# SwiGLU's transposed result: from TensorE transposes to VectorE block transposes and GpSimd moves in 13 of 22 blocks

## The chip, the cores and the metric

One core of a Trainium2 chip runs the kernel. The metric is device time in microseconds (us), the median of repeated runs. Five engines matter: PE (TensorE, matmuls), DVE (VectorE), ACT (ScalarE), POOL (GpSimd) and SP (SyncE, which issues the loads). Each works through its own queue in the order in which the instructions stand there, and waits at an instruction until what it needs is done.

## The reference

One decoder layer on 256 tokens of width 2048: a SwiGLU half step, a mixing layer, another SwiGLU half step, each with norms and a conditioning vector. Cut to what the change touches:

```python
D_MODEL = 2048; SEQ = 256; D_FF = 5632

def swiglu(h, w_gate, w_up, w_down):
    return (jax.nn.silu(h @ w_gate) * (h @ w_up)) @ w_down
# x: (1, 256, 2048) float32; gate and up: (2048, 5632), down: (5632, 2048), all float32
```

The conditioning vector is multiplied with `w_ada` (2048 x 18432), a stream of its own beside the layer's weights.

## The kernel before

**Tiles.** All products keep float32 accuracy by three matmuls (`mm3`): a value is split into a rounded high part and a rest, and high times high, high times rest and rest times high are added in PSUM. A weight tile is 512 KB (2 x 128 rows of 512 columns). `load_w` has SP load it into one of 8 slots of the pool `rawp` (tag `raw`); `split_w` has ACT cast it to `wh` (L315) and DVE subtract to get `wl` (L320), into one of 4 pairs. PE then runs 12 matmuls of it (2 row halves, 2 token halves, 3 products), lines L338 to L340. A slot of `rawp` is free once the subtraction has read it. The tiles of `w_ada` use the same 8 slots; DVE accumulates them (L172).

**Blocks.** A feed-forward step (FFN0 at the start, FFN1 at the end) has 11 blocks of 512 hidden columns. A block runs gate's tiles, then up's tiles, both with the 128 tokens of a half on partitions, into two PSUM banks each (`gb[t]`, `ub[t]`). Blocks are grouped into supers; after the blocks of a super come its tiles of `w_down`. FFN0's supers are blocks 8, 5, 6, 7; then 0, 1, 2, 3; then 4, 9, 10. FFN1's are 4, 4 and 3 blocks. Most blocks have 16 row tiles of 128, that is 8 weight tiles for gate and 8 for up. In FFN0 blocks 0 to 4 some of the rows were done earlier and their sums lie in SBUF (`part`): 12 rows are left, 6 tiles for gate and 6 for up, and `swiglu_sum` adds the stored part. `swiglu_evac` does the other blocks.

**SwiGLU's result.** For each token half t, ACT takes Silu of gate and DVE multiplies by up. In `swiglu_evac` Silu (L551) reads gate's PSUM bank, and DVE multiplies (L552). In `swiglu_sum` DVE first adds the stored part to gate (L564), ACT takes Silu (L565), DVE adds the stored part to up (L566) and multiplies (L567). The down product needs this with hidden columns on partitions, so `to_g` transposes: 8 PE transposes of 128x128 (L542), in two groups of four, each group into one PSUM bank, from which ACT casts (L373) and DVE subtracts (L374).

**What sets the order.** Steps that are to run beside the weight stream are generators in `pending`; one step runs after each weight tile (`pump`). A tile scheduler then settles each engine's order, bound by data and by `behind(instruction, other)`, which keeps an instruction after another on its engine. `floor[0]` (DVE) and `floor[1]` (ACT) name the instruction that every later `wl` and `wh` must stand behind.

Of the kernel before, what the change touches and what calls it, by code (L numbers as in the profile page):

```python
# [8 lines left out]
F32 = mybir.dt.float32  # L9
F32R = mybir.dt.float32r  # L10
AF = mybir.ActivationFunctionType
# [3 lines left out]
P = 128  # L15
D = 2048
S = 256
NT = S // P
# [14 lines left out]
def tile_layer(  # L33
# [6 lines left out]
    nc = tc.nc  # L40
# [14 lines left out]
    rawp = ctx.enter_context(tc.tile_pool(name="rawp", bufs=8))  # L55
# [9 lines left out]
    def nm(s):  # L65
        uid[0] += 1
        return f"{s}_{uid[0]}"

    def ps():
        return psp.tile([P, 512], F32, tag="ps", name=nm("ps"))  # L70

    def t2(shape=(P, 512), dtype=F32):
        return tp.tile(list(shape), dtype, tag="t2", name=nm("t2"))
# [63 lines left out]

    last_split = [None]
    first_splits = [2]
    floor = [None, None]  # L140
    last_update = [None]

    def behind(ins, other):

        if other is not None:
            tc.add_manual_dep(ins.ins, other.ins.name, mybir.DependencyInfo(
                mybir.DependencyClass.NoSync, mybir.DependencyReason.DATA), reason="order")
# [129 lines left out]
    pending = []  # L277
# [17 lines left out]
    def flush():  # L295
        while pending:
            pump()
# [10 lines left out]
    def split_w(rawv, slot, w):  # L308
        if slot is None:
            wh = wsp.tile([P, 2, 512], F32R, tag="wh", name=nm("wh"))  # L310
            wl = wsp.tile([P, 2, 512], F32R, tag="wl", name=nm("wl"))
        else:
            wh, wl = slot[:, 0], slot[:, 1]
        wh, wl = wh[:, :, 0:w], wl[:, :, 0:w]
        behind(nc.scalar.copy(wh, rawv), floor[1])  # L315
        if first_splits[0]:
            first_splits[0] -= 1
            nc.gpsimd.tensor_tensor(out=wl, in0=rawv, in1=wh.bitcast(F32), op=ALU.subtract)
            return wh, wl
        last_split[0] = nc.vector.tensor_tensor(out=wl, in0=rawv, in1=wh.bitcast(F32), op=ALU.subtract)  # L320
        behind(last_split[0], floor[0])
        return wh, wl
# [49 lines left out]
    def split_act(dh, dl, src):  # L372
        act = nc.scalar.copy(dh, src)  # L373
        return nc.vector.tensor_tensor(out=dl, in0=src, in1=dh.bitcast(F32), op=ALU.subtract), act  # L374


    def parts():

        p = small((P, 8), "parts")
        nc.gpsimd.memset(p[:, 3:4], EPS)  # L380
        return p
# [151 lines left out]
        return banks, 2  # L533


    def to_g(g, gts):
        for i in range(2):
            pg = ps()
            for j in range(2):
                for t in range(NT):  # L540
                    m = 2 * i + j
                    nc.tensor.transpose(pg[:, j * S + t * P:j * S + (t + 1) * P], gts[t][:, m * P:(m + 1) * P], ident)  # L542
            split_act(g.t[:, 0, 2 * i:2 * i + 2, :], g.t[:, 1, 2 * i:2 * i + 2, :],
                      pg.rearrange("p (k s) -> p k s", s=S))
            yield

    def swiglu_evac(g, gb, ub):
        gts = []
        for t in range(NT):
            sg, gt = t2(), t2()  # L550
            nc.scalar.activation(sg, gb[t], AF.Silu)  # L551
            nc.vector.tensor_tensor(out=gt, in0=sg, in1=ub[t], op=ALU.mult)  # L552
            gts.append(gt)
        yield
        yield
        yield from to_g(g, gts)

    def swiglu_sum(gb, ub, part):

        pv = part.t.rearrange("p k s -> p (k s)")  # L560
        gts = []
        for t in range(NT):
            sg, gt = t2(), t2()
            nc.vector.tensor_tensor(out=sg, in0=pv[:, t * 512:(t + 1) * 512], in1=gb[t], op=ALU.add)  # L564
            nc.scalar.activation(sg, sg, AF.Silu)  # L565
            nc.vector.tensor_tensor(out=gt, in0=pv[:, 1024 + t * 512:1024 + (t + 1) * 512], in1=ub[t], op=ALU.add)  # L566
            nc.vector.tensor_tensor(out=gt, in0=sg, in1=gt, op=ALU.mult)  # L567
            gts.append(gt)
        part.free()
        g = Slot((P, 2, 4, S), F32R)  # L570

        def rest():
            yield
            yield
            yield from to_g(g, gts)

        pending.append(rest())
        return g

    def ffn(idx, supers, begun, xin, nxt, nxt_src=None, nxt_c0=None, nxt_w=512):  # L580

        y = None
        yp = [parts() for _ in range(NT)]

        def evac_y(si, q, t, bank):
            ys = y[t].t[:, q * 512:(q + 1) * 512]
            if si == 0:
                nc.scalar.copy(ys, bank)
            else:
                nc.vector.tensor_tensor(out=ys, in0=ys, in1=bank, op=ALU.add)  # L590
            if si == len(supers) - 1:
                sumsq(yp[t], q, ys)

        for si, blocks in enumerate(supers):
            gs = []
            n = len(blocks)
            for b, segs, part, banks in blocks:
                if si == 0 and begun is not None and not gs:
                    gb = proj_tok(w_ff_gate[idx], b * FB, begun)
                    ub = proj_tok(w_ff_up[idx], b * FB)  # L600
                elif part is not None:
                    gb = proj_tok(w_ff_gate[idx], b * FB, segs=segs, first=segs[0][0])
                    ub = proj_tok(w_ff_up[idx], b * FB, segs=segs, first=segs[0][0])
                    flush()
                    gs.append(swiglu_sum(gb, ub, part))
                    continue
                else:
                    gb = proj_tok(w_ff_gate[idx], b * FB, segs=segs, banks=banks and banks[0])
                    ub = proj_tok(w_ff_up[idx], b * FB, segs=segs, banks=banks and banks[1])
                flush()  # L610
                gs.append(Slot((P, 2, 4, S), F32R))
                pending.append(swiglu_evac(gs[-1], gb, ub))
            if y is None:
                y = [Slot((P, D)) for _ in range(NT)] if xin[0].__class__ is Half else [Half(t) for t in range(NT)]
            rows = [(4 * i, 4, 4 * b[0]) for i, b in enumerate(blocks)]

            def mms(k, wh, wl, t):
                g = gs[k // 4].t
                mm3(banks[t], g[:, 0, k % 4, t * P:(t + 1) * P], g[:, 1, k % 4, t * P:(t + 1) * P],
                    wh, wl, k == 0, k == 4 * n - 1)  # L620

            for q in range(4):
                banks = [ps(), ps()]
                if si == len(supers) - 1 and q == 2:
                    for s_ in xin:
                        s_.t
                if si == len(supers) - 1 and q == 3:
                    flush()
                    if side[0] is not None:
                        side[0].drain()  # L630
                    early = early_w(nxt_src, nxt_c0, nxt_w)
                    kept, slots = hold(w_ff_down[idx], rows, q * 512, NW if nxt is None else 3)

                    def last_mm(t):
                        for k, wh, wl in kept:
                            mms(k, wh, wl, t)

                    return boundary(last_mm, lambda t: evac_y(si, q, t, banks[t]), lambda t: times_gg(y, t, q), xin, y, yp, slots + gs,
                                    early, 1, nxt, nxt_src, nxt_c0, nxt_w)
                else:  # L640
                    for k, wh, wl in w_tiles(w_ff_down[idx], rows, q * 512):
                        for t in range(NT):
                            mms(k, wh, wl, t)
                    for t in range(NT):
                        later(evac_y, si, q, t, banks[t])
                        if si == len(supers) - 1:
                            later(times_gg, y, t, q)
            if si < len(supers) - 1:
                for g in gs:
                    g.free()  # L650
# [68 lines left out]
    for bs, n in (((0, 1, 2, 3, 4), 1), ((5, 6), 2), ((7,), 3)):  # L719
        first.until(n - 1)  # L720
        for b in bs:
            part = Slot((P, 8, S))
# [5 lines left out]
    banks = [proj_tok(gate_up[u], 8 * FB, segs=FULL[:3]) for u in range(2)]  # L728
# [25 lines left out]

    blocks = [(4718, 410), (4308, 410), (3896, 412), (3484, 412), (G0, 412)]
    begun = ffn(0, supers, None, xin, 1, w_in, *blocks[0])
    side[0] = None

# [58 lines left out]
    for i, (c0, w) in enumerate(blocks):  # L817
        banks = proj_tok(w_in, c0, begun if i == 0 else None, w)
# [147 lines left out]
    for i in range(2):  # L966
        banks = proj_t(w_in, i * 512)
# [72 lines left out]
    for i in range(2):  # L1040
        banks = proj_tok(w_in, O0 + i * 512)
# [44 lines left out]
    for q in range(4):  # L1086
        banks = b0 if q == 0 else [ps(), ps()]
# [55 lines left out]
```

## Time and profile before

| what | value |
|---|---|
| median of 3 runs | 1872.48 us (1872.23 to 1872.91) |
| the profiled execution, whole time | 1872.83 us |
| its span from first to last instruction | 1870.8 us |
| PE busy | 1823.0 us, 97% of the span |
| DVE busy | 1365.0 us |
| ACT busy | 853.6 us |
| POOL busy | 22.5 us |

Times of rows are microseconds from the span's start. An engine's row gives when an instruction began, how long it took, its line and its tiles, and in brackets how long the engine was idle before it and what ended that. Rows begin a little before the preceding one ends where the engine takes them in as a pipeline, so the step from start to start is what a sequence costs.

### The profile page before, as it was taken

Reading aid. Unit: us, or ns where it says so; the run is one execution under the profiler, and the core shown is the slowest. Engines: PE = TensorE matmul, PEld = TensorE weight load, DVE = VectorE, ACT = ScalarE, POOL = GpSimd, SP = SyncE. Lnnn points to the kernel's source line nnn. Section 1 sums busy time; section 2 is a strip of 40 time slices with the busy share of each in tenths; the row PEclk is TensorE's granted clock in tenths of the full one; section 3 lists DMA queues with packets and bytes.
Section 4 is the critical chain, followed back from the end, with each engine's and each line's share of the span. In section 5 each row is a group of like instructions: output and inputs, shape, how many; then the busy total and the mean of one; then the engine's idle time right before and its main releaser. Section 6 shows DMA issues by size and latency. Waiting matters only on the chain.

```text
span 1870.8 us, 23057 instructions
## 1 busy us (share of the span) xinstructions
PE 1823.0 (97%) x8501; PEld 1523.7 (81%) x8501; DVE 1365.0 (73%) x1479; ACT 853.6 (46%) x1058; POOL 22.5 (1%) x42
## 2 busy tenths in 40 slices
PE   3999999999999999999999999999999999999998
PEld 2888888888888888799988887888888888888886
DVE  6888798788987888868898987555556555556455
ACT  3555444444443444655545446444444444334443
POOL 1000000000000000000000000000000000000000
PEclk9999999999999999999999999999999999999999
DMA  9999889999899999578689994776677776677662
GB/s 346 346 359 342 314 293 318 319 307 322 294 331 323 340 306 334 188 240 278 218 288 306 358 342 141 221 223 213 228 228 221 221 223 214 219 228 220 190 190 91
DMA packets 232617, 499.82 MB, mean 267 GB/s; under 512 B 16828, under 2 KB 28332, under 8 KB 231992
## 3 DMA queue, kind: packets, MB, share of 16 engines
q1 hardware_dynamic: 232504, 498.36, 79.9%
q8 instruction: 66, 1.08, 0.2%
q14 instruction: 47, 0.39, 0.1%
HBM read 496.19 MB, written 2.10 MB: 266 GB/s over the span
## 4 chain that ended last, share of the span: by engine, by line
PE 86%; issue 8%; DVE 3%; DMA 2%; POOL 1%; ACT 0%; DVEq 0%; POOLq 0%; ACTq 0%; SPq 0%
PE ps L338 28%; PE ps L339 28%; PE ps L340 28%; DVE acc L172 2%; PE ps L542 1%; DVE wl L320 1%; DMA raw<-in_w_ada_dram 1%; DMA raw<-in_w_ff_up_dram 0%; POOL rstd L391 0%; DMA raw<-in_w_ff_gate_dram 0%; DMA xt<-in_x_dram 0%; PE ps L197 0%; PE ps L930 0%; ACT wh L315 0%; POOL brs L808 0%
## 5 line engine op out<-in xcount | busy, mean ns | idle before, releaser
L320 DVE TENSOR_TENSOR wl<-raw,wh 128x1024 fp32r<-128x1024 f32 (+2 forms) x635 | 766.1, 1210 | 450.3 <-ACT wh L315 449.3
L315 ACT CAST wh<-raw 128x1024 fp32r<-128x1024 f32 (+2 forms) x637 | 662.6, 1043 | 864.1 <-PE ps L340 737.0
L338 PE MATMUL ps<-wh,hh 128*128 128x512 f32 (+2 forms) x1680 | 650.3, 390 | 1.5 <-ACT hh L373 1.5
L339 PE MATMUL ps<-wl,hh 128*128 128x512 f32 (+2 forms) x1680 | 649.3, 387 | 1.2 <-DVE wl L320 1.2
L340 PE MATMUL ps<-wh,hl 128*128 128x512 f32 (+2 forms) x1680 | 649.1, 386 | 0.0
L339 PEld LDWEIGHTS ps<-wl,hh 128*128 128x128 f32 x1680 | 316.5, 188 | 61.9 <-DVE wl L320 2.7
L340 PEld LDWEIGHTS ps<-wh,hl 128*128 128x128 f32 x1680 | 316.1, 188 | 60.5
L338 PEld LDWEIGHTS ps<-wh,hh 128*128 128x128 f32 x1680 | 315.9, 188 | 60.1 <-ACT hh L373 1.7
L172 DVE SCALAR_TENSOR_TENSOR acc<-raw,cs,acc 128x1024 f32<-128x1024 f32 x270 | 345.1, 1278 | 0.8 <-DVE parts L389 0.4
L338 PE MATMUL ps<-wh,big 128*128 128x512 f32 x804 | 314.6, 392 | 0.0
L339 PE MATMUL ps<-wl,big 128*128 128x512 f32 x804 | 313.1, 389 | 0.2 <-DVE wl L320 0.2
L340 PE MATMUL ps<-wh,big 128*128 128x512 f32 x804 | 313.1, 389 | 0.0
L339 PEld LDWEIGHTS ps<-wl,big 128*128 128x128 f32 x804 | 151.0, 188 | 31.8 <-DVE wl L320 1.0
L340 PEld LDWEIGHTS ps<-wh,big 128*128 128x128 f32 x804 | 150.9, 188 | 31.7
L338 PEld LDWEIGHTS ps<-wh,big 128*128 128x128 f32 x804 | 150.9, 188 | 30.6
L338 PE MATMUL ps<-hh,wh 128*128 128x256 f32 x128 | 37.6, 293 | 0.0
L680 ACT COPY big<-ps 128x512 f32<-128x512 f32 x32 | 18.7, 589 | 40.8 <-PE ps L340 39.5
L374 DVE TENSOR_TENSOR big<-ps,big 128x512 fp32r<-128x512 f32 x52 | 35.5, 683 | 1.3 <-ACT big L373 1.2
L340 PE MATMUL ps<-hh,wl 128*128 128x256 f32 x128 | 36.2, 283 | 0.0
L339 PE MATMUL ps<-hl,wh 128*128 128x256 f32 x128 | 36.2, 283 | 0.0
L373 ACT CAST big<-ps 128x512 fp32r<-128x512 f32 x52 | 30.1, 578 | 0.0
L385 ACT ACTIVATE t<-xt 128x512 f32<-128x512 f32 x32 | 20.0, 626 | 17.7 <-DVE xt L590 9.6
(194 smaller groups left out, 751.4 us busy)
## 6 DMA issues: line engine op xcount, KB each, us to landing
raw<-in_w_ada_dram SPq DMA_DIRECT2D x224, 512.0 KB, 5.3
raw<-in_w_ff_gate_dram SPq DMA_DIRECT2D x176, 512.0 KB, 4.5
raw<-in_w_ff_up_dram SPq DMA_DIRECT2D x176, 512.0 KB, 4.5
raw<-in_w_ff_down_dram SPq DMA_DIRECT2D x176, 512.0 KB, 5.1
raw<-in_w_ada_dram SPq DMA_DIRECT2D x128, 256.0 KB, 5.5
raw<-in_w_in_dram SPq DMA_DIRECT2D x48, 512.0 KB, 5.1
raw<-in_w_out_dram SPq DMA_DIRECT2D x32, 512.0 KB
raw<-in_w_in_dram SPq DMA_DIRECT2D x24, 412.0 KB, 4.8
```

Source lines behind the costliest of these rows:

```text
L172: ins = nc.vector.scalar_tensor_tensor(a, raw[:, j, :, :], cs[:, k:k + 1], a, op0=ALU.mult, op1=ALU.add)
L315: behind(nc.scalar.copy(wh, rawv), floor[1])
L320: last_split[0] = nc.vector.tensor_tensor(out=wl, in0=rawv, in1=wh.bitcast(F32), op=ALU.subtract)
L338: nc.tensor.matmul(o, lh, rh, start=start, stop=False, skip_group_check=True)
L339: nc.tensor.matmul(o, lh, rl, start=False, stop=False, skip_group_check=True)
L340: nc.tensor.matmul(o, ll, rh, start=False, stop=stop, skip_group_check=True)
L373: act = nc.scalar.copy(dh, src)
L374: return nc.vector.tensor_tensor(out=dl, in0=src, in1=dh.bitcast(F32), op=ALU.subtract), act
L385: nc.scalar.activation(junk, src, AF.Square, scale=float(D) ** -0.5, accum_out=p[:, q + q // 3:q + q // 3 + 1])
L542: nc.tensor.transpose(pg[:, j * S + t * P:j * S + (t + 1) * P], gts[t][:, m * P:(m + 1) * P], ident)
L680: nc.scalar.copy(part.t.rearrange("p k s -> p (k s)")[:, u * 1024 + i * 512:u * 1024 + (i + 1) * 512], banks[i])
```

## The change

For a block whose successor in the same super has at least 12 row tiles, the PE transposes are replaced: DVE transposes each token half in 32x32 squares into a tile `tr`, and POOL moves the squares to their places in a tile `gf` by 16 copies of 32 partitions x 256 elements. Both tiles come from `rawp`, tag `raw`, so they take two of the 8 load slots. Nine steps of `pending` later ACT and DVE split `gf` from SBUF as they did PSUM. These are 13 of the 22 blocks: in FFN0 0, 1, 2 and 4 (by `swiglu_sum`) and 9 (by `swiglu_evac`), in FFN1 eight (by `swiglu_evac`). In these blocks both floors are set: later weight casts stand behind the second Silu, later weight residuals behind the second square transpose.

```diff
-        behind(nc.scalar.copy(wh, rawv), floor[1])
+        last_cast[0] = nc.scalar.copy(wh, rawv)
+        behind(last_cast[0], floor[1])
...
+    def to_g_blocks(g, gts):
+        tr = rawp.tile([P, NT, 4, 4, 32], F32, tag="raw", name=nm("tr"))
+        gf = rawp.tile([P, 4, NT, 4, 32], F32, tag="raw", name=nm("gf"))
+        for t in range(NT):
+            floor[0] = nc.vector.transpose(tr[:, t].rearrange("p m q r -> p (m q r)"), gts[t])
+        for b in range(4):
+            for q in range(4):
+                nc.gpsimd.tensor_copy(gf[q * 32:(q + 1) * 32, :, :, b, :].rearrange("p m t r -> p t m r"),
+                                      tr[b * 32:(b + 1) * 32, :, :, q, :])
+        for _ in range(9):
+            yield
+        for i in range(2):
+            sub, cast = split_act(g.t[:, 0, 2 * i:2 * i + 2, :], g.t[:, 1, 2 * i:2 * i + 2, :],
+                                  gf[:, 2 * i:2 * i + 2].rearrange("p m t b r -> p m (t b r)"))
+            behind(cast, last_cast[0])
+            behind(sub, last_split[0])
+            yield
...
-    def swiglu_evac(g, gb, ub):
+    def swiglu_evac(g, gb, ub, blocks):
...
-            nc.scalar.activation(sg, gb[t], AF.Silu)
+            silu = nc.scalar.activation(sg, gb[t], AF.Silu)
...
+        if blocks:
+            floor[1] = silu
         yield
-        yield
-        yield from to_g(g, gts)
+        if blocks:
+            yield from to_g_blocks(g, gts)
+        else:
+            yield
+            yield from to_g(g, gts)
...
-    def swiglu_sum(gb, ub, part):
+    def swiglu_sum(gb, ub, part, blocks):
...
-            nc.scalar.activation(sg, sg, AF.Silu)
+            silu = nc.scalar.activation(sg, sg, AF.Silu)
...
+        if blocks:
+            floor[1] = silu
...
-            for b, segs, part, banks in blocks:
+            for i, (b, segs, part, banks) in enumerate(blocks):
+                slow = i + 1 < n and sum(nk for _, nk, _ in blocks[i + 1][1]) >= 12
```

The lines of the changed file differ: the cast is L316, the residual L322, the accumulation L173, the loads L305 and L158, Silu L592 (sum) and L573 (evac), the sums L591 and L593, the products L594 and L574, the square transposes L544, POOL's copies L547, the split L375 and L376.

**ACT, end of FFN0's block 0 and start of block 1.** `raw_660_3230` is block 0's last up tile, `raw_671_3266` block 1's first gate tile, and `t2_666` the gate half that the second Silu works on. Before:

```order
L315 CAST wh_661_3232<-raw_660_3230 128x1024
L315 CAST wh_672_3268<-raw_671_3266 128x1024
L315 CAST wh_676_3289<-raw_675_3287 128x1024
L315 CAST wh_679_3307<-raw_678_3305 128x1024
L315 CAST wh_684_3335<-raw_683_3333 128x1024
L565 ACTIVATE t2_666_3257<-t2_666_3257 128x512
```

After:

```order
L316 CAST wh_661_3232<-raw_660_3230 128x1024
L592 ACTIVATE t2_666_3257<-t2_666_3257 128x512
L316 CAST wh_672_3268<-raw_671_3266 128x1024
L316 CAST wh_676_3289<-raw_675_3287 128x1024
L316 CAST wh_681_3327<-raw_680_3325 128x1024
```

The second Silu moved ahead of the casts of block 1's first four gate tiles.

**DVE at the same place.** `ps_640` and `ps_641` are the two banks of block 0's up product, `ps_617` a bank of its gate product; `wl_673`, `wl_677` and `wl_680` (after: `wl_682`) are residuals of block 1's first three gate tiles. Before:

```order
L320 TENSOR_TENSOR wl_677_3290<-raw_675_3287,wh_676_3289 128x1024
L320 TENSOR_TENSOR wl_680_3308<-raw_678_3305,wh_679_3307 128x1024
L566 TENSOR_TENSOR t2_665_3252<-big_45_256,ps_640_3129 128x512
L564 TENSOR_TENSOR t2_666_3257<-big_45_256,ps_617_3006 128x512
L567 TENSOR_TENSOR t2_665_3252<-t2_664_3251,t2_665_3252 128x512
L566 TENSOR_TENSOR t2_667_3258<-big_45_256,ps_641_3130 128x512
```

After:

```order
L593 TENSOR_TENSOR t2_665_3252<-big_45_256,ps_640_3129 128x512
L591 TENSOR_TENSOR t2_666_3257<-big_45_256,ps_617_3006 128x512
L594 TENSOR_TENSOR t2_665_3252<-t2_664_3251,t2_665_3252 128x512
L593 TENSOR_TENSOR t2_667_3258<-big_45_256,ps_641_3130 128x512
L544 STREAM_TRANSPOSE tr_678_3305<-t2_665_3252 128x512
L594 TENSOR_TENSOR t2_667_3258<-t2_666_3257,t2_667_3258 128x512
L322 TENSOR_TENSOR wl_673_3269<-raw_671_3266,wh_672_3268 128x1024
L173 SCALAR_TENSOR_TENSOR acc_588_2869<-raw_663_3249,cs_107,acc_588_2869 128x1024
L322 TENSOR_TENSOR wl_677_3290<-raw_675_3287,wh_676_3289 128x1024
L544 STREAM_TRANSPOSE tr_678_3305<-t2_667_3258 128x512
L322 TENSOR_TENSOR wl_682_3328<-raw_680_3325,wh_681_3327 128x1024
```

All residuals of block 1 now stand behind block 0's last sum and products; the third stands behind the second square transpose.

**SP, the loads around the same place, after** (block 1's gate tiles in order are 3266, 3287, 3325, 3346, 3367, 3385):

```order
L305 DMA raw_684_3346<-in_w_ff_gate_dram 128x2x512 [waits DMAHW4_49,DMAHW1_49,DVE_49]
L158 DMA raw_687_3365<-in_w_ada_dram 128x1024 [waits DMAHW3_49,DVE_49]
L305 DMA raw_688_3367<-in_w_ff_gate_dram 128x2x512 [waits DMAHW6_49,DVE_49]
L305 DMA raw_691_3385<-in_w_ff_gate_dram 128x2x512 [waits DVE_49,Pool_49]
L158 DMA raw_695_3405<-in_w_ada_dram 128x1024 [waits DMAHW7_49,DMAHW5_49,DVE_49]
L305 DMA raw_698_3409<-in_w_ff_up_dram 128x2x512 [waits DVE_49]
```

Block 1's sixth gate tile (3385) takes the slot of `tr`: its load now waits for POOL's copies, and every later load stands behind it; before, no load of this stretch waited for POOL. So it is in all 13 blocks: the load that waits for POOL is the next block's sixth gate tile in FFN0's five, its seventh in five of FFN1's, its eighth in two (in one of them a `w_ada` tile just ahead of it waits first), and its first up tile in the last one.

**DVE, end of a block in FFN1** (`ps_2053` and `ps_2054` are the block's two up banks; `wl_2085`, `wl_2092`, `wl_2097`, `wl_2100` belong to the next block's first four gate tiles). Before:

```order
L320 TENSOR_TENSOR wl_2154_10725<-raw_2152_10722,wh_2153_10724 128x1024
L320 TENSOR_TENSOR wl_2157_10743<-raw_2155_10740,wh_2156_10742 128x1024
L552 TENSOR_TENSOR t2_2149_10715<-t2_2148_10714,ps_2114_10541 128x512
L552 TENSOR_TENSOR t2_2151_10719<-t2_2150_10718,ps_2115_10542 128x512
L320 TENSOR_TENSOR wl_2161_10768<-raw_2159_10765,wh_2160_10767 128x1024
```

After, one block earlier:

```order
L322 TENSOR_TENSOR wl_2085_10435<-raw_2083_10432,wh_2084_10434 128x1024
L574 TENSOR_TENSOR t2_2087_10451<-t2_2086_10450,ps_2053_10276 128x512
L574 TENSOR_TENSOR t2_2089_10455<-t2_2088_10454,ps_2054_10277 128x512
L544 STREAM_TRANSPOSE tr_2093_10476<-t2_2087_10451 128x512
L322 TENSOR_TENSOR wl_2092_10461<-raw_2090_10458,wh_2091_10460 128x1024
L544 STREAM_TRANSPOSE tr_2093_10476<-t2_2089_10455 128x512
L322 TENSOR_TENSOR wl_2097_10499<-raw_2095_10496,wh_2096_10498 128x1024
L322 TENSOR_TENSOR wl_2100_10517<-raw_2098_10514,wh_2099_10516 128x1024
```

Before, three residuals of the next block stood ahead of the products; after, one does, and the second and third stand beside the square transposes.

## Rows read from the trace of the kernel before

**Rows 1.** Page: busy us, share, instructions; granted PE clock in 40 slices (tenths).

```profile
PE 1823.0 (97%) x8501; PEld 1523.7 (81%) x8501; DVE 1365.0 (73%) x1479; ACT 853.6 (46%) x1058; POOL 22.5 (1%) x42
...
PEclk9999999999999999999999999999999999999999
```

**Rows 2.** Groups by line: busy us, mean ns of one, idle before, releasers.

```profile
L183 DVE STREAM_TRANSPOSE t<-acc 128x512 f32<-128x512 f32 x22 | 14.6, 692 | 0.1
```

**Rows 3.** Timeline of ACT in FFN1, with both groups of transposes; start, duration, instruction.

```profile
1269.57 1.05 ACT L315 CAST wh<-raw 128x1024 fp32r<-128x1024 f32 x1 [1.66 <-PE ps L340]
1272.29 1.05 ACT L315 CAST wh<-raw 128x1024 fp32r<-128x1024 f32 x1 [1.67 <-PE ps L340]
...
1275.50 1.05 ACT L315 CAST wh<-raw 128x1024 fp32r<-128x1024 f32 x1 [1.68 <-PE ps L340]
...
1278.69 1.05 ACT L315 CAST wh<-raw 128x1024 fp32r<-128x1024 f32 x1 [1.65 <-PE ps L340]
```

**Rows 4.** Timeline of ACT, FFN0 block 0 to block 1.

```profile
391.86 1.05 ACT L315 CAST wh<-raw 128x1024 fp32r<-128x1024 f32 x1 [1.67 <-PE ps L340]
...
399.98 1.06 ACT L315 CAST wh<-raw 128x1024 fp32r<-128x1024 f32 x1 [1.67 <-PE ps L340]
400.94 0.63 ACT L565 ACTIVATE t<-t 128x512 f32<-128x512 f32 x1
```

**Rows 5.** Timeline of DVE, the same place.

```profile
398.34 1.22 DVE L320 TENSOR_TENSOR wl<-raw,wh 128x1024 fp32r<-128x1024 f32 x1 [1.49 <-ACT wh L315]
399.48 0.68 DVE L566 TENSOR_TENSOR t<-big,ps 128x512 f32<-128x512 f32 x1
400.08 0.68 DVE L564 TENSOR_TENSOR t<-big,ps 128x512 f32<-128x512 f32 x1
```

**Rows 6.** Timeline of PE: the first two matmuls of block 1.

```profile
399.77 0.39 PE L338 MATMUL ps<-wh,hh 128*128 128x512 f32 x1
400.00 0.39 PE L339 MATMUL ps<-wl,hh 128*128 128x512 f32 x1
```

**Rows 7.** Timeline of POOL: fills and selects.

```profile
0.80 0.20 POOL masks.py:197 MEMSET ident<- 128x128 f32 x1 [0.29 <-POOLq L1130]
0.94 0.20 POOL L104 MEMSET onesr<- 128x128 f32 x1
1.18 0.29 POOL masks.py:199 TENSOR_SCALAR_AFFINE_SELECT ident<-ident 128x128 f32<-128x128 f32 x1
1.42 0.10 POOL L108 MEMSET nhalf<- 128x8 f32 x1
...
895.75 1.18 POOL L891 TENSOR_SCALAR_AFFINE_SELECT t<-t 128x512 f32<-128x512 f32 x1 [43.31 <-DMA raw<-in_w_in_dram]
907.81 0.64 POOL L891 TENSOR_SCALAR_AFFINE_SELECT t<-t 128x512 f32<-128x512 f32 x1 [10.88 <-DMA raw<-in_w_in_dram]
```

**Rows 8.** Timeline of DVE beside POOL's two last rows.

```profile
895.74 0.68 DVE L898 TENSOR_TENSOR t<-t,t 128x512 f32<-128x512 f32 x1
...
907.94 1.05 DVE L898 TENSOR_TENSOR t<-t,t 128x512 f32<-128x512 f32 x1
```

**Rows 9.** DMA issues between 1200 and 1300 us: KB each, median us to landing.

```profile
raw<-in_w_ff_gate_dram SPq DMA_DIRECT2D x15, 512.0 KB, 3.5
```

**Rows 10.** Timelines of DVE and of PE, FFN0 block 4 to block 9.

```profile
624.20 1.28 DVE L232 SCALAR_TENSOR_TENSOR big<-ps,t 128x512 f32<-128x512 f32 x2
...
624.21 0.39 PE L339 MATMUL ps<-wl,hh 128*128 128x512 f32 x1
```

**Rows 11.** Timeline of DVE, end of a block in FFN1.

```profile
1263.64 1.28 DVE L552 TENSOR_TENSOR t<-t,ps 128x512 f32<-128x512 f32 x2
```

**Rows 12.** Timeline of PE at the start, after a wait of 15.9 us.

```profile
38.16 0.63 PE L339 MATMUL ps<-wl,hh 128*128 128x512 f32 x1
38.58 0.63 PE L340 MATMUL ps<-wh,hl 128*128 128x512 f32 x1
...
43.27 0.56 PE L339 MATMUL ps<-wl,hh 128*128 128x512 f32 x1
```

More of the change, by code (lines that the diff above doesn't have):

```diff
@@ L139, in tile_layer @@
     first_splits = [2]
+    last_cast = [None]
     floor = [None, None]
@@ L573, in rest @@
             yield
-            yield
-            yield from to_g(g, gts)
+            if blocks:
+                yield from to_g_blocks(g, gts)
+            else:
+                yield
+                yield from to_g(g, gts)
         pending.append(rest())
@@ L604, in ffn @@
                     flush()
-                    gs.append(swiglu_sum(gb, ub, part))
+                    gs.append(swiglu_sum(gb, ub, part, slow))
                     continue
@@ L611, in ffn @@
                 gs.append(Slot((P, 2, 4, S), F32R))
-                pending.append(swiglu_evac(gs[-1], gb, ub))
+                pending.append(swiglu_evac(gs[-1], gb, ub, slow))
             if y is None:
```

## The prediction

> **What bounds the kernel now.** I read the busy shares first: PE works 1823.0 of 1870.8 us, DVE 1365.0, POOL 22.5 [rows 1]. So PE is the bound, and a change helps only if it takes work out of PE's queue without making PE wait. Then I read ACT's timeline in FFN1 for the pace: casts start 2.72 us apart, each released by PE, which has just freed the pair of a tile four back [rows 3]. One period is 12 matmuls. The periods with a group of four transposes are 3.21 and 3.19 us long. Last I read the passage from one block to the next. There PE goes from block 0 to block 1 of FFN0 without a gap [rows 6], because block 1's first tile was cast at 391.86, eight microseconds before PE wanted it [rows 4], and the third residual was begun at 398.34, before the sums of block 0 [rows 5]. This lead, three to four tiles, is what keeps PE at 97%.
>
> **What the change takes away.** Two groups of transposes per block lengthen two periods by 0.49 and 0.47 us [rows 3], so a block gives 0.96 us. 13 blocks give **12.5 us**, 4.8 in FFN0 and 7.7 in FFN1. The split of the result (ACT's cast, DVE's subtraction) only changes its source and stands ten tiles later; I put it at nothing, as ACT has idle time ahead of every cast [rows 3] and the down product needs the result much later. If that cover failed, a cast would be late by less than a microsecond against a lead of eight.
>
> **What it puts on PE's path, first: the order at FFN0's block ends.** In four of the FFN0 blocks (0, 1, 2, 4) the second Silu waits for a DVE sum that stands behind the sum of up's first bank, and that needs the block's last matmuls. Before, ACT had cast four tiles of the next block ahead of that Silu; now all of them stand behind it, and DVE's residuals behind the sums and products. I follow it in the times of block 0. The up sum starts at 399.48, the gate sum at 400.08 and takes 0.68 [rows 5]. Silu takes 0.63 from about 400.9, the first cast of block 1 1.05, so it ends at 402.6 [rows 4]. Meanwhile DVE runs the first product, up's second sum, a square transpose (0.69 [rows 2]) and the second product, which waits for Silu; at 0.6 a step it is through at about 403.1. The first residual takes 1.2 and ends at 404.3. PE's second matmul of block 1 needs it; now it starts at 400.00 [rows 6]. **4.3 us** each at blocks 0, 1 and 2. At block 4 PE's second matmul of the next block starts at 624.21, and DVE has two steps of 0.64 first that need PE's work from just before it [rows 10]; I let them start half a microsecond before that matmul and end by 624.9. Then come two sums, a product and a sum (0.6 each, 627.3), the transpose (628.0), the last product (628.6) and the residual (629.8): **5.6 us**. Sum 3 x 4.3 + 5.6 = 18.5 us. This is more than the whole gain. It rests on the queue order alone, not on an unknown price. In FFN1 and at block 9 Silu reads gate's banks, done long before; there the second tile's residual comes behind two products (1.28 together [rows 11]) and one transpose: about 2.7 us after PE's last matmul, wanted at 2.9. I put that at zero.
>
> **Second: POOL's copies and the load behind them.** `tr` holds a load slot until 16 copies are done; a gate tile of the next block waits for that slot, and SP's queue with all later loads waits behind it. No row has such a copy. From below: a fill of 128 elements a partition takes 0.20, starts 0.14 after the one before it, and one of 8 takes 0.10, so 256 elements take at least 0.24 start to start. From above: a select takes 0.29 at 128 and 0.64 at 512 elements, so 0.41 at 256 [rows 7]. I take 0.30, nearer to the fill, because a copy has no comparison; 16 copies are 4.8 us (3.8 to 6.6).
>
> They don't run alone. A select that started 0.01 us after a DVE instruction with two SBUF inputs took 1.18 instead of 0.64; a DVE instruction of that kind that started during a select took 1.05 instead of 0.68 [rows 7, 8]. In each pair the later one stood until the first ended. DVE's residuals and accumulations all have two SBUF inputs, about 1.2 us apiece [rows 5]. The Trainium skill, page "SBUF — State Buffer", section "Who interferes with whom", says that a DVE instruction with two SBUF inputs and a GpSimd instruction that reads SBUF exclude one another, whoever comes first holding the port for its whole length. By that rule copies belong to this case too, which no row shows.
>
> So I add the two. After the second square transpose DVE has five such instructions before it lacks tiles: 6.0 us (six at blocks 4 and 9: 7.4). Counted in FFN0 from the first residual's end at 404.3: an accumulation, a residual and the transpose bring POOL's start to 407.3; 4.8 + 6.0 later, 418.1, the slot is free. The load lands in 3.5 [rows 9], cast, residual and steps between take 2.4, so the sixth tile is ready at 424.0. PE wants it five tiles after 404.3, at 417.9. **6.1 us** at blocks 0, 1, 2. The same for block 4: start 631.7, ready 649.8, wanted 643.4: 6.4. Block 9, from PE's last matmul: start 3.5, ready 21.6, wanted 13.8: 7.8. In FFN1: start 3.4, ready 20.1. Five blocks want the tile (their seventh) at 16.5: 3.6 each; two (the eighth) at 19.2: 0.9 each; the last, a ninth, at 22.0: nothing. Sum: 18.3 + 6.4 + 7.8 + 18.0 + 1.8 = 52.3 us.
>
> **Sum.** -12.5 + 18.5 + 52.3 = +58.3 on the profiled 1872.83 us, 1931.1; the median lies 0.35 below the profiled execution, so **1931 us**. With copies of 0.24 it is 1919, with 0.41, 1953.
>
> **Rivals.**
> 1. POOL's copies slip between DVE's work at their own length, with no exclusion that matters. Then the tile is ready 6.0 to 7.4 us earlier: FFN1 waits for nothing, FFN0 0.7 us in all. 1872.5 - 12.5 + 18.5 + 0.7 = 1879 (1887 with copies of 0.41). For it: DVE stands idle ahead of a residual (1.49 us, [rows 5]), time in which a copy meets nobody; against it: the pairs of [rows 7, 8].
> 2. Faster: the passage of blocks in FFN0 does not stop PE, since the lead that ACT and DVE had is made up, and the copies end in time. Then only the gain is left, 1860. It decides at 3.1 us a passage, where four of them eat the gain. Against it stands the order of both queues.
> 3. PE's clock falls in the waits. At the start, after a wait, matmuls started 0.42 us apart (38.16, 38.58, and so on to 43.27) where they elsewhere start 0.23 apart [rows 6, 12], which is the lower level, 1.2 GHz, for the upper, 2.4: some 13 matmuls, 2.5 us. With 16 waits (four passages, twelve loads) up to 40 us more: 1971. For it: the waits are of 4 to 8 us; against it: some are broken by a matmul, and the page shows the granted clock at full in every slice, the first too [rows 1], so that only the pace speaks for it. The Trainium skill, page "TensorE: Matmul & The Clock Gate", section "HAM oscillation — how this bites in real kernels", tells of a kernel whose clock went back to half in every wait for a load. By that rule the time is this rival's; no row here has such a wait in the middle of the weight stream.
>
> That the change doesn't do what it says is no case: 104 of 176 transposes leave PE's queue.
>
> **How the numbers follow.** Chances: forecast 0.50 (1919 to 1953); rival 1, or copies that exclude only in part, 0.24 (1877 to 1915); rival 3, 0.08; rival 2, 0.12; gain and loss that cancel within 0.2% (3.7 us, about what a measurement of this kernel can tell from no change) 0.06. The range leaves out rival 2 and the upper half of rival 3: 1872 to 1962. Faster 0.12, within 0.2% 0.06, slower 0.82.
>
> **What would show it.** The timeline of ACT at FFN0's block ends should show Silu, then the first cast of the next block after PE has stopped; PE should wait there for a cast and then for a residual, about 4 us. POOL's copies should be 0.24 to 0.41 us alone and stretched beside DVE; DVE's residuals some 0.3 longer there. SP's load of the sixth (FFN1: seventh) gate tile should be issued right after the last copy, and PE should wait for its cast. FFN1's blocks should be shorter by 0.96 where no such wait is. I am wrong on the first step if PE runs through at FFN0's passages, and on the second if the copies end within about 7 us of their start.

## The result, and the profile after

The changed kernel takes 1971.62 us (median of 4 runs, 1970.07 to 1972.54) against 1872.70 before (1872.23 to 1872.99): ratio 1.0527, 95% interval 1.0514 to 1.0539, 98.9 us slower. The forecast was 1931, slower, with a range up to 1962: the sign held, the size did not.

Page, busy us and share, and the granted clock by slices, as [rows 1]; then the group of POOL's copies (busy us, mean ns | idle before, releaser):

```profile
PE 1855.2 (94%) x8397; PEld 1535.5 (78%) x8397; DVE 1385.5 (70%) x1505; ACT 851.3 (43%) x1058; POOL 167.7 (9%) x250
...
PEclk9999999988899899999999999999999999999999
...
L547 POOL COPY gf<-tr 32x256 f32<-32x256 f32 x208 | 145.2, 698 | 1219.3 <-DVE tr L544 1177.0
```

PE has 104 matmuls fewer and is busy 32 us longer. The clock line has dents, in the slices of FFN0's second and third supers, where [rows 1] had none. What PE waited for (us in all, times, longest) is new:

```profile
PE ps L340 <- ACT wh L316: 53.4, 16, 6.8
...
PE ps L341 <- DVE wl L322: 12.9, 22, 1.3
```

Sixteen waits for a cast: four at FFN0's block ends, twelve at a late gate tile, five of them in FFN0 and seven in FFN1. PE at FFN0's block 0 to block 1, with the sixth tile of block 1 below (columns: start, duration, line, operands, idle before and what ended it):

```profile
398.29 0.39 PE L342 MATMUL ps<-wh,hl 128*128 128x512 f32 x1
400.97 0.73 PE L340 MATMUL ps<-wh,hh 128*128 128x512 f32 x2 [2.29 <-ACT wh L316]
402.90 0.78 PE L341 MATMUL ps<-wl,hh 128*128 128x512 f32 x1 [1.20 <-DVE wl L322]
403.47 0.63 PE L342 MATMUL ps<-wh,hl 128*128 128x512 f32 x1
...
417.56 0.39 PE L342 MATMUL ps<-wh,hl 128*128 128x512 f32 x1
422.25 0.80 PE L340 MATMUL ps<-wh,hh 128*128 128x512 f32 x1 [4.29 <-ACT wh L316]
423.51 0.80 PE L341 MATMUL ps<-wl,hh 128*128 128x512 f32 x1 [0.47 <-DVE wl L322]
424.10 0.63 PE L342 MATMUL ps<-wh,hl 128*128 128x512 f32 x1
424.53 0.63 PE L340 MATMUL ps<-wh,hh 128*128 128x512 f32 x1
```

Where [rows 6] had no gap, the first residual's matmul starts 4.6 us after the block's last one, and the matmuls that follow both waits start 0.43 us apart instead of 0.23. What the others did there: ACT's second Silu with the casts behind it, and the cast that waits for its load; DVE's first residual of the block; POOL's 16 copies; SP's load of the sixth tile (two loads in one row, the second issued at its end):

```profile
399.35 0.63 ACT L592 ACTIVATE t<-t 128x512 f32<-128x512 f32 x1 [10.42 <-DVE t L591]
399.89 2.92 ACT L316 CAST wh<-raw 128x1024 fp32r<-128x1024 f32 x3
...
421.15 1.04 ACT L316 CAST wh<-raw 128x1024 fp32r<-128x1024 f32 x1 [10.03 <-DMA raw<-in_w_ff_gate_dram]
```

```profile
401.63 1.22 DVE L322 TENSOR_TENSOR wl<-raw,wh 128x1024 fp32r<-128x1024 f32 x1
```

```profile
405.93 11.51 POOL L547 COPY gf<-tr 32x256 f32<-32x256 f32 x16 [364.13 <-DVE tr L544]
...
1287.64 11.38 POOL L547 COPY gf<-tr 32x256 f32<-32x256 f32 x16 [38.24 <-DVE tr L544]
```

```profile
405.20 12.63 SPq L305 DMA_DIRECT2D raw<-in_w_ff_gate_dram  x2
```

Against [rows 4] the Silu now has idle time ahead of it and the casts behind it; the copies end at 417.44, the load goes out behind them, and its tile is cast at 421.15. Both steps of the forecast are in the trace, at the places it named.

Where the time is lost: POOL's last small row ahead of FFN1 stood at 1132.79 (first row) and stands at 1191.41, so FFN0 lost 58.6 us. The spans of the two profiled executions differ by 1968.0 - 1870.8 = 97.2 us (the medians by 98.9), so FFN1 lost the remaining 38.6.

```profile
1132.79 0.55 POOL L391 TENSOR_TENSOR rstd<-parts,nhalf 128x1 f32<-128x1 f32 x1 [6.01 <-DVE parts L389]
...
1191.41 0.55 POOL L393 TENSOR_TENSOR rstd<-parts,nhalf 128x1 f32<-128x1 f32 x1 [6.02 <-DVE parts L391]
```

### The profile page after: what moved, and what is told of

Its sections match the earlier page's. It is cut to its first block, busy times and chain, and to the rows that moved or that the text cites. A ratio compares the mean times of both kernels' runs of the same rounds, so it can differ in the third digit from the quotient of the medians.

```text
span 1968.0 us, 23123 instructions
## 1 busy us (share of the span) xinstructions
PE 1855.2 (94%) x8397; PEld 1535.5 (78%) x8397; DVE 1385.5 (70%) x1505; ACT 851.3 (43%) x1058; POOL 167.7 (9%) x250
## 5 line engine op out<-in xcount | busy, mean ns | idle before, releaser
L322 DVE TENSOR_TENSOR wl<-raw,wh 128x1024 fp32r<-128x1024 f32 (+2 forms) x635 | 769.8, 1219 | 449.0 <-ACT wh L316 444.9
L316 ACT CAST wh<-raw 128x1024 fp32r<-128x1024 f32 (+2 forms) x637 | 660.4, 1042 | 904.9 <-PE ps L342 536.3
L340 PE MATMUL ps<-wh,hh 128*128 128x512 f32 (+2 forms) x1680 | 657.4, 397 | 54.9 <-ACT wh L316 53.4
L341 PE MATMUL ps<-wl,hh 128*128 128x512 f32 (+2 forms) x1680 | 666.1, 397 | 12.9 <-DVE wl L322 12.8
L342 PE MATMUL ps<-wh,hl 128*128 128x512 f32 (+2 forms) x1680 | 661.5, 394 | 0.0
L340 PEld LDWEIGHTS ps<-wh,hh 128*128 128x128 f32 x1680 | 323.7, 193 | 123.3 <-ACT wh L316 59.9
L341 PEld LDWEIGHTS ps<-wl,hh 128*128 128x128 f32 x1680 | 324.5, 193 | 85.9 <-DVE wl L322 23.4
L342 PEld LDWEIGHTS ps<-wh,hl 128*128 128x128 f32 x1680 | 324.3, 193 | 61.6
L173 DVE SCALAR_TENSOR_TENSOR acc<-raw,cs,acc 128x1024 f32<-128x1024 f32 x270 | 347.1, 1285 | 0.9 <-DVE parts L391 0.5
L547 POOL COPY gf<-tr 32x256 f32<-32x256 f32 x208 | 145.2, 698 | 1219.3 <-DVE tr L544 1177.0
L574 DVE TENSOR_TENSOR t<-t,ps 128x512 f32<-128x512 f32 x28 | 18.8, 685 | 39.6 <-PE ps L342 39.1
L393 POOL TENSOR_TENSOR rstd<-parts,nhalf 128x1 f32<-128x1 f32 x12 | 7.6, 631 | 342.0 <-DVE parts L391 342.0
```

Source lines behind the costliest of these rows:

```text
L173: ins = nc.vector.scalar_tensor_tensor(a, raw[:, j, :, :], cs[:, k:k + 1], a, op0=ALU.mult, op1=ALU.add)
L316: last_cast[0] = nc.scalar.copy(wh, rawv)
L340: nc.tensor.matmul(o, lh, rh, start=start, stop=False, skip_group_check=True)
L341: nc.tensor.matmul(o, lh, rl, start=False, stop=False, skip_group_check=True)
L342: nc.tensor.matmul(o, ll, rh, start=False, stop=stop, skip_group_check=True)
L393: nc.gpsimd.tensor_tensor(out=r, in0=p[:, 6:7], in1=nhalf[:, 0:1], op=ALU.pow)
```

## Experiments

My theory after the result: four waits from the Silu floor, twelve from `tr`'s load slot, and matmuls at half pace behind them. All ratios are to runs of the kernel before on the same chip.

### Taking the waits away, one cause at a time, and the clock by itself

The first edit takes out the ACT floor, in `swiglu_sum` and in `swiglu_evac`.

```diff
-        if blocks:
-            floor[1] = silu
```

> The changed kernel without the line that makes later weight casts stand behind the second Silu; everything else as changed. Theory: the four waits at FFN0's block ends (blocks 0, 1, 2, 4) come from that line, about 3.5 us of waiting plus some 2 us at the lower clock each, so about 23 us go: 1971.6 to about 1949. Rival: the residuals' own order on VectorE makes those waits, and the casts only share them; then under 5 us go. The twelve waits for a load stay in both.

Measured: 1948.92 us, ratio 1.0401 (1.0385 to 1.0416): 22.7 us less, the number of the theory, but not where the theory had it. At block 0 PE runs through the block end; the only wait left there is the one for the load, and it is longer than before:

```profile
419.14 0.79 PE L340 MATMUL ps<-wh,hh 128*128 128x512 f32 x1 [6.91 <-ACT wh L316]
```

So a wait at the block end is for the most part given back at the load, where PE that comes sooner waits longer: its idle time at FFN0's five load waits went from 23.2 to 35.3 us. POOL's row ahead of FFN1 stands at 1185.08, so of the 20.6 us between the two profiled executions FFN0 gained 6.3 us, and FFN1, where no PE wait stood at a block end, 14.3:

```profile
1185.08 0.55 POOL L393 TENSOR_TENSOR rstd<-parts,nhalf 128x1 f32<-128x1 f32 x1 [6.01 <-DVE parts L391]
```

What changed in FFN1 is the place of the square transposes. In the seven blocks ahead of a wait DVE ran a weight residual between the two of them; without the floor they follow each other, POOL starts 1.1 us sooner after the products, and so does the load behind it. The same block in the changed kernel and in this one:

```profile
1234.49 0.71 DVE L544 STREAM_TRANSPOSE tr<-t 128x512 f32<-128x512 f32 x1
1235.12 1.18 DVE L322 TENSOR_TENSOR wl<-raw,wh 128x1024 fp32r<-128x1024 f32 x1
1236.22 0.70 DVE L544 STREAM_TRANSPOSE tr<-t 128x512 f32<-128x512 f32 x1
```

```profile
1228.17 1.30 DVE L544 STREAM_TRANSPOSE tr<-t 128x512 f32<-128x512 f32 x2
```

PE's idle time at FFN1's load waits fell from 19.4 to 13.2 us, and less of the half pace followed. That the total met the theory is luck; what the four waits cost by themselves, the next two kernels tell.

The second edit keeps `tr`'s slot until the split, so that no load waits for the copies.

```diff
         for _ in range(9):
             yield
+        behind(nc.scalar.copy(held, tr[:, 0, 0, 0, 0:1]), last_cast[0])
```

> The changed kernel with a one-element read of tr at the time of the split, so that tr's load slot is given back ten tiles later: no load of the next block's gate waits for POOL any more, and six slots serve the loads meanwhile. The waits at FFN0's block ends stay. Theory: the twelve waits for a load vanish with the lower clock behind them: 97 + 12.5 us lost in all, less 23 for the passages, so about 86 us go: about 1886. Rival: six slots are too few beside w_ada's stream, and PE waits for loads elsewhere; then over 1915.

Measured: 1888.70 us, ratio 1.0082 (1.0065 to 1.0099): 82.9 us less. The load of the sixth tile no longer stands behind the copies, though these take longer, 14.8 us where they took 11.5:

```profile
405.80 2.10 SPq L306 DMA_DIRECT2D raw<-in_w_ff_gate_dram  x2
```

```profile
406.52 14.77 POOL L548 COPY gf<-tr 32x256 f32<-32x256 f32 x16 [364.62 <-DMA raw<-in_w_ff_gate_dram]
```

Six slots are enough here; the copies' own length costs nothing, once no load waits for their end. The four waits at block ends are left (2.29, 2.14, 2.29 and 4.14 us of idle time for the cast). The row ahead of FFN1 stands at 1155.12:

```profile
1155.12 0.55 POOL L394 TENSOR_TENSOR rstd<-parts,nhalf 128x1 f32<-128x1 f32 x1 [6.01 <-DVE parts L392]
```

> Both edits together. Theory: no wait is left and the transposes are gone from PE: 1872.7 - 12.5, about 1860 to 1864. Rival (VectorE and GpSimd shut each other out so long that residuals come late, or six slots are too few): 1872 or more.

Measured with both edits: 1866.96 us, ratio 0.9968 (0.9955 to 0.9981), faster than before. Its row ahead of FFN1:

```profile
1135.06 0.55 POOL L394 TENSOR_TENSOR rstd<-parts,nhalf 128x1 f32<-128x1 f32 x1 [6.01 <-DVE parts L392]
```

Against the second kernel FFN0 is 20.1 us shorter and FFN1 0.6: with no load to wait for, this is what the Silu floor costs, and it lies where the theory had it. The gains of the single edits add up in the total (22.7 + 82.9 = 105.6, together 104.7), but not by place: in the profiled executions FFN0 gains 6.3 + 36.3 against 56.4 together, FFN1 14.3 + 44.8 against 45.4. No wait for a cast is left; of the 7 us missing to 1860, 3.4 are new waits for residuals. The view counts 4.5; four of its seven waits (0.26, 0.26, 0.42 and 0.21) stand in the kernel before too:

```profile
PE ps L342 <- DVE wl L323: 4.5, 7, 1.6
```

The two longest stand at FFN0's block 4 to block 9, 1.63 and 1.30 us; the first edit alone had them there too.

The fourth kernel leaves all waits and fills fifteen of the sixteen (the shortest, 0.60 us, stays empty) with matmuls into an unused bank, held in place on PE's queue:

```diff
+            f = nc.tensor.matmul(bank, onesr, hh[:, 0:2, :].rearrange("p k s -> p (k s)"), start=True, stop=True,
+                                 skip_group_check=True)
+            behind(f, last_mm3[0])
...
+    FILL = {(0, 1, 0): {0: 16, 5: 20}, (0, 1, 1): {0: 16, 5: 18}, (0, 1, 2): {0: 16, 5: 20},
+            (0, 2, 0): {0: 18, 5: 19}, (0, 2, 1): {5: 30},
+            (1, 0, 0): {7: 12}, (1, 0, 1): {6: 14}, (1, 0, 2): {6: 14},
+            (1, 1, 0): {6: 13}, (1, 1, 2): {6: 14}, (1, 2, 0): {7: 11}}
```

(Step, super and block ahead of the wait; then the tile in the next gate and the number of matmuls.)

> The changed kernel with matmuls whose result nobody uses put in front of the tile for which PE waits, 11 to 30 of them, a little less than the wait is long; the waits themselves stay. Theory: the matmuls after each wait run at the lower clock because PE stood idle, some 45 us in all; with PE kept at work most of it is saved: 1971.6 to about 1930 to 1940. Rival: the slow pace belongs to the tiles that come late (their data), or the added matmuls take PE's time: 1970 or more.

Measured: 1950.67 us, ratio 1.0413 (1.0398 to 1.0429). 20.9 us come back, half of what I expected. The same places: the filler and the first matmuls behind it, at the block end, at the sixth tile, and at a late tile in FFN1.

```profile
399.36 3.89 PE L370 MATMUL ps<-hh,onesr 128*128 128x512 f32 x16
403.09 0.62 PE L340 MATMUL ps<-wh,hh 128*128 128x512 f32 x2
403.75 0.49 PE L341 MATMUL ps<-wl,hh 128*128 128x512 f32 x1
...
417.02 4.83 PE L370 MATMUL ps<-hh,onesr 128*128 128x512 f32 x20
423.17 0.50 PE L340 MATMUL ps<-wh,hh 128*128 128x512 f32 x1 [1.33 <-ACT wh L316]
424.43 0.79 PE L341 MATMUL ps<-wl,hh 128*128 128x512 f32 x1 [0.76 <-DVE wl L322]
...
1248.22 2.96 PE L370 MATMUL ps<-hh,onesr 128*128 128x512 f32 x12
1251.13 0.49 PE L340 MATMUL ps<-wh,hh 128*128 128x512 f32 x1
1252.39 0.50 PE L341 MATMUL ps<-wl,hh 128*128 128x512 f32 x1 [0.77 <-DVE wl L322]
1252.73 0.39 PE L342 MATMUL ps<-wh,hl 128*128 128x512 f32 x1
1252.96 0.39 PE L340 MATMUL ps<-wh,hh 128*128 128x512 f32 x1
```

Granted clock and PE busy in stretches of the changed kernel and, below, of the filled one (columns: stretch, its length, busy us of PE, PEld, DVE, ACT, POOL, granted clock, DMA share, GB/s):

```profile
400.00:407.00 7.00, 4.83 (x13) 3.57 (x14) 7.00 (x9) 3.25 (x4) 1.07 (x1) 0.76 0.40 130
407.00:417.50 10.50, 10.50 (x48) 8.69 (x47) 5.14 (x4) 1.67 (x2) 9.82 (x16) 1.00 0.17 64
417.50:427.00 9.50, 4.74 (x12) 3.10 (x12) 4.74 (x5) 2.67 (x3) 0.00 (x0) 0.64 0.92 333
```

```profile
400.00:407.00 7.00, 6.96 (x30) 5.38 (x30) 7.00 (x10) 3.47 (x4) 0.23 (x1) 1.00 0.31 87
417.50:427.00 9.50, 7.42 (x26) 5.45 (x25) 3.82 (x5) 2.09 (x2) 0.62 (x2) 0.85 0.83 296
```

The clock is shown: with PE at work through the wait the granted clock stays at its upper level (1.00 where it was 0.76), and matmuls behind it start 0.23 us apart. In the changed kernel 15 stretches behind waits run at the lower pace, 132 steps of 0.43 us, 26.8 us more than at the upper pace; in the filled one two such stretches are left, 2.4 us, at 425 and 685, behind 1.33 and 1.44 us in which the filler had ended and the cast was not there (1.63 and 1.31 us at two other places left none). My 45 us were wrong twice. I had taken the whole rise of PE's busy time for the clock, but the matmuls at a wait are shown busy for up to 0.80 us (422.25 and 423.51 above), part of which counts among the waits. And FFN0 gives back little: the row that stood at 1191.41 stands at 1186.94,

```profile
1186.94 0.55 POOL L415 TENSOR_TENSOR rstd<-parts,nhalf 128x1 f32<-128x1 f32 x1 [6.01 <-DVE parts L413]
```

4.5 us, with nine filled waits; FFN1's six give 15.6. In FFN0 a faster PE reaches the sixth tile sooner and waits there longer: 4.8 + 1.3 us of filler and idle time at 417 against 4.3. The residual's matmul of block 1's sixth tile stands 25.3 us behind block 0's last matmul (399.13), in the changed kernel 25.2.

### Are copies and VectorE in each other's way

```diff
+                if 0 < b * 4 + q < 15:
+                    move = nc.gpsimd.memset(o, 0.5)
+                else:
+                    move = nc.gpsimd.tensor_copy(o, tr[b * 32:(b + 1) * 32, :, :, q, :])
+                behind(move, last_move)
```

> The changed kernel, in which 14 of POOL's 16 copies are fills of the same 32 x 256 elements, which write gf and read nothing from SBUF (so most of the SwiGLU result is left out and replaced by a constant in these blocks); the first and the last stay copies, the order and the load behind them stay. Theory: POOL's batch takes 11 to 13 us because copies and VectorE's instructions with two SBUF inputs shut each other out; fills don't, so a batch takes 4 to 6 us, the load is issued some 6 us sooner, FFN1's waits vanish and FFN0's become short: 1971.6 to about 1890. Rival: POOL's instructions of this shape are slow in themselves beside any work; the batch stays over 9 us and the time over 1940.

Measured: 1898.98 us, ratio 1.0143 (1.0128 to 1.0159). POOL at block 0, and DVE at the same time:

```profile
406.68 1.23 POOL L552 COPY gf<-tr 32x256 f32<-32x256 f32 x1 [364.84 <-DMA raw<-in_w_ff_gate_dram]
407.95 4.76 POOL L550 MEMSET gf<- 32x256 f32 x14
412.76 0.58 POOL L552 COPY gf<-tr 32x256 f32<-32x256 f32 x1
```

```profile
408.92 1.21 DVE L322 TENSOR_TENSOR wl<-raw,wh 128x1024 fp32r<-128x1024 f32 x1
410.05 1.27 DVE L173 SCALAR_TENSOR_TENSOR acc<-raw,cs,acc 128x1024 f32<-128x1024 f32 x1
```

Fourteen fills take 4.76 us, 0.34 each, while DVE runs without a gap; the copy ahead of them, beside the same work, takes 1.23. A copy that meets nobody takes 0.39 (the least and the middle of 208 in the changed kernel are 390 and 397 ns; the longest is 2489). The changed kernel's batch at block 0 shows both: five copies beside five of DVE's instructions with two SBUF inputs, then eleven, which start 0.43 us apart, after DVE has run out of tiles:

```profile
405.93 6.70 POOL L547 COPY gf<-tr 32x256 f32<-32x256 f32 x5 [364.13 <-DVE tr L544]
```

```profile
412.68 4.77 POOL L547 COPY gf<-tr 32x256 f32<-32x256 f32 x11
```

With fills the batch is 6.7 us instead of 11.5, a little over the expected 4 to 6, and in FFN1 no wait for a load is left. The time is 9 us above the expected 1890; block 9's load still makes PE wait, 1.81 us for the cast.

### The new way where it pays

On top of both edits:

```diff
-                slow = i + 1 < n and sum(nk for _, nk, _ in blocks[i + 1][1]) >= 12
+                slow = idx == 1 and i + 1 < n and sum(nk for _, nk, _ in blocks[i + 1][1]) >= 12
```

> The kernel with both edits (no Silu floor, tr's slot held until the split), and the new way in FFN1's eight blocks alone; FFN0 keeps its PE transposes. Theory: FFN1 gives its full 8 x 0.96 = 7.7 us, and FFN0, where VectorE and the loads are fuller, gave a loss: 1872.7 - 7.7, about 1865. Rival: both halves gain in the version with both edits; then this one is slower than 1867.0 by what FFN0 gave, about 1869.

Measured: 1864.48 us against 1872.45, ratio 0.9958 (0.9945 to 0.9970), the fastest of all. From the row ahead of FFN1 to the end it takes 1862.2 - 1131.85 = 730.35 us where the kernel before takes 1870.8 - 1132.79 = 738.01:

```profile
1131.85 0.55 POOL L394 TENSOR_TENSOR rstd<-parts,nhalf 128x1 f32<-128x1 f32 x1 [6.02 <-DVE parts L392]
```

That is 7.7 us for eight blocks, the price that the forecast read off two periods. POOL's batches there are 12.4 to 15.4 us long and nobody waits for them. In FFN0 the version with both edits has this row at 1135.06, 3.2 us later. So FFN0 gives its 4.8 us and loses 8.0: 3.4 are the waits for residuals, 1.0 is a stretch at the lower pace at 1130 us, far from the blocks, behind idle times of 1.36 and 0.81 us that the kernel before has too, without such a stretch; the rest I have not placed.

## Why the prediction was right and wrong, step by step

- **The gain, 0.96 us a block:** right. FFN1 gave 7.7 us for eight blocks as soon as nothing waited.
- **The Silu at FFN0's block ends, 18.5 us:** right. From the last matmul of block 0 (398.29) to the first residual's (402.90) are 4.6 us, of which 0.7 are the steps of the three starts between; so 3.9 against 4.3, and 3.5, 3.9 and 5.7 at the others, 17.0 in all. Without the line, and with no load to wait for, FFN0 is 20.1 us shorter, half pace included. The 22.7 us of the first edit (20.6 between the profiled executions) are not this price: 14.3 arose in FFN1, where the forecast put the order at nothing. PE hardly waited there for it (0.66 us, once), but with it the second square transpose, and POOL behind that, came 1.1 us later.
- **POOL's copies and the load, 52.3 us:** the mechanism was right to the tile. The batch was 11.4 to 12.4 us in FFN0, forecast 10.8 to 12.2; that this came so near is partly luck. Copies alone start 0.43 us apart, where I took 0.30 and at most 0.41, so 16 are 6.9 us and not 4.8; and VectorE lengthened the batch by 4.5 us, not by 6.0 (5.4 at blocks 4 and 9, not 7.4). PE's waits for these loads, counted in the same way, are 29.2 us in FFN0 (forecast 32.5) and 27.8 in FFN1 (forecast 19.8). FFN1 was too low for two reasons. The batch was longer by 0.6 us, and landing and cast came later than 5.9 us after it: copies end at 1299.02, the residual's matmul starts at 1305.38, 6.4 us. With the start at 3.4 and a batch of 11.4 the tile is ready 21.1 us after PE's last matmul, not 20.1, and a seventh tile waits 4.6 us, not 3.6. And I had miscounted: four blocks want their seventh tile and three their eighth, not five and two (so also in the part on the change); the three eighths waited 4.0, 1.8 and 3.8 us, where the sum had 0.9. That the first of them stands behind a tile of `w_ada` I had set at nothing; in the third the batch took 13.5 us.
- **All waits together:** 74.0 us measured, 70.8 in the sum. Had this been all, the time would have been about 1934.
- **The step that failed: the clock.** I had it as a rival at 0.08, priced at 2.5 us a wait, and put zero into the sum. It fell behind 15 of the 16 waits: 26.8 us more at the lower pace, of which 20.9 us came back with the waits filled. The Trainium skill, page "TensorE: Matmul & The Clock Gate", section "HAM oscillation — how this bites in real kernels", tells of a kernel whose clock went back to half in its waits for loads, and the traces agree, with a granted clock of 0.76 and 0.64 in the two stretches shown. The reasons I gave against it did not hold: two matmuls in the middle of a wait (2.29 and 1.20 us at the block end) did not keep the clock up, and the granted clock of the page before was at full because that kernel had no such waits after its start: behind 44 us PE's longest idle time there is 1.4 us. Rival 3's time, 1971, is near the result by luck: it had 2.5 us a wait, 40 in all, where the lower pace took 26.8 us and 1.3 us a wait came back. The rest of the difference is in the next point.
- **What stays open:** between the profiled executions 12.5 + 97.2 = 109.7 us were lost; 74.0 of waits and 26.8 of pace make 100.8. At the same sixteen places 6.9 us more stand: the step behind a late residual's matmul is 0.57 to 0.59 us (402.90 to 403.47, 423.51 to 424.10), some 0.36 above 0.23 at fifteen of them and 0.11 at the sixteenth, 5.5 in all, and the steps in which the pace rises make 1.3. About 2.0 us stay open.
- **Rival 1** (no exclusion) fell with the fills, **rival 2** (faster) with the first trace. Both of the kernel's parts can be had without their waits, and then the change gains; the forecast said nothing of that.

## What to carry to other kernels

A slow engine's tile in a pool that in-order loads share puts that engine on the path of every later load; ask of each new tile who takes its slot next, and when. A wait on PE cost its own length here and, behind 15 of 16, some matmuls at half pace; put the second into the sum with the first. And an instruction that is set ahead of the weight casts takes the lead that hides them: 4 us of waiting for that order is four times the 0.96 us that a block gains. Last, where an experiment gives back the number you expected, look where in the trace the time came back: the first edit's 22.7 us matched the theory, and more than half of them came from another place.

## What the runs showed of the hardware

- A GpSimd copy of 32 partitions x 256 float32 took 0.39 us, 0.43 from start to start; a fill of the same shape 0.34 from start to start. Beside VectorE instructions with two SBUF inputs a copy took up to 2.5 us (1.2 to 1.4 at block 0) and 16 copies 11 to 19; fourteen fills beside them took 4.8 to 5.2 in all 13 blocks. The Trainium skill, page "SBUF — State Buffer", section "Who interferes with whom", says that such a VectorE instruction contends with a GpSimd instruction that reads SBUF, not with one that only writes it, and the runs agree.
- VectorE lost less by it than GpSimd: its residuals and accumulations, 1.2 to 1.3 us by themselves, took 1.45 at most beside copies, where a copy went from 0.39 to 1.2 and more.
- After a wait of 2.3 and 1.2 us with two matmuls between, PE already ran at the lower of its two levels (granted clock 0.76 from 400 to 407), for six further matmuls; after FFN1's waits of 2.6 to 3.5 us, for 10 to 13.
